# The first mixer's three streams of conditioning weights start behind the input projection's fourth block

## The chip, the core and the metric

One core of a Trainium2 chip runs the whole kernel. The metric is device time of one execution in microseconds (us). The engines are named as in the profile: PE (matmuls), PEld (PE's weight loads), DVE (vector), ACT (scalar activation), POOL (GpSimd) and SP, which issues the DMA loads. Each engine works through its own list of instructions in a fixed order and waits on semaphores for what the others produce.

## What is computed

A decoder trunk of two layers on 256 tokens of width 1024. A layer is a token mixer behind an input projection, then a feed-forward part (dense in the first layer, two of eight experts in the second). Six vectors per layer, made from one conditioning vector, modulate both parts:

```python
cond = silu(c)
for layer in range(2):
    mod = cond @ ada_w[layer] + ada_b[layer]
    shift_mix, scale_mix, gate_mix, shift_ffn, scale_ffn, gate_ffn = split(mod, 6)
    a = rms_norm(h, norm_mix_g[layer]) * (1 + scale_mix) + shift_mix
    z = a @ w_in[layer]        # columns: conv | s5 | stick-breaking | nsa
    h = h + gate_mix * (concat[conv(z), s5(z), stick(z), nsa(z)] @ w_out[layer])
    a = rms_norm(h, norm_ffn_g[layer]) * (1 + scale_ffn) + shift_ffn
    h = h + gate_ffn * (swiglu(a) if layer == 0 else top2of8_swiglu(a))
```

`shift_mix` and `scale_mix` are needed before the input projection. `gate_mix`, `shift_ffn` and `scale_ffn` (the products (0, 2), (0, 3) and (0, 4) below) are needed only behind the first mixer. The s5 part is a linear recurrence: a projection of the state input, two scans over time, an output projection, a gelu and a gate.

## The kernel before

The weight `w_in` is worked through in eleven column blocks of 256. One block is 48 products of 128x128 by 256 (fp32 split into a high and a low part, so three products for each of 16 tiles: lines 291, 292 and 293). Its weights come in one load of 1 MB, of which each half is rounded to the high part on ACT (`wh`) and subtracted on DVE (`wl`, 128x1024); the result stands in a PSUM bank. The pool of PSUM tiles that is called "ps" has two banks, and from the fifth block on every block takes one of them in turn; the pool "acc" has six, for everything else. There are nine buffers for loaded weights (`raw`), four for `wh` and three for `wl`.

Beside the blocks run side streams, Python generators in the list `sides`. `drive(main, sides)` steps each of them once at every `yield` of the main stream, so that they are recorded in small pieces between the products. The main stream of the first mixer writes blocks 0 to 3 (0 is the s5 input), then blocks 6, 7, 4, 5, 8, 9, 10 (`ORDER`), each with four yields. The streams that matter here:

- `s5()`: DVE and ACT copy block 0 into the layout of the recurrence (line 639); 16 small matmuls (line 644) into two banks; on DVE four products, two sums, the scans (lines 656 and 657) and six products and sums that end in the tiles H[0] and H[1]; 24 matmuls into one bank (line 674 on the input, line 676 on H[0] and H[1]); then gelu on ACT, copies on DVE and ACT (line 689), and a gate (line 695 and following).
- `compress()`, `rope()`, `gates()`: other parts of the mixer. `compress()` has its own loads, 32 matmuls (line 732), an activation on ACT and DVE, and two transposes (line 745).
- `extra`: for the first mixer one generator that waits three yields and then makes the three conditioning vectors (0, 2), (0, 3) and (0, 4). Each has four loads of 1 MB (`in_ada_w`), eight fp32 matmuls per load (line 360) and, behind the fourth, an evacuation and a turn into a column (lines 341 to 352, matmuls on line 348). In all 12 loads, 12 MB, and 96 matmuls. For the second mixer `extra` holds the sums for the router (lines 1116 to 1121).

`EV` says which engine empties a block's bank behind it: block 6 ACT, block 7 DVE, block 4 ACT. What is recorded is not yet the order: a scheduler sorts each engine's instructions, and the program is then fixed. Loads are issued by SP in its own order, and one that needs a `raw` buffer still in use holds those behind it.

Of the kernel before, what the change touches and what calls it, by code (L numbers as in the profile page):

```python
# [167 lines left out]
def trunk(ctx: ExitStack, tc: tile.TileContext, I, out):  # L168
# [15 lines left out]
    def s2(shape, dt=F32):  # L184
        return st(shape, "s2", NS2, dt)

    def bank(tag="acc"):
        return ps.tile([128, 512], F32, tag=tag, bufs=NPS[tag], name=nm(tag))
# [13 lines left out]
    def act(o, a, f, **k):  # L202
        S.activation(o, a, f, **k)  # L203
# [27 lines left out]
    def P(l, n, lo=0, hi=None):  # L231
        o, w = SP[n]
        s_, o = (spa[:, l], o) if o < NSA else (sps[l], o - NSA)
        return s_[:, o + lo:o + (w if hi is None else hi)]
# [66 lines left out]
    def run(*gens):  # L301
        for g in gens:
            for _ in g:
                pass

    def drive(main, sides):

        for _ in main:
            for g in list(sides):
                if next(g, 0) == 0:  # L310
                    sides.remove(g)
        while sides:
            for g in list(sides):
                if next(g, 0) == 0:
                    sides.remove(g)
# [254 lines left out]
    def hop(n, l):  # L570
        for _ in range(1 + PAUSE.get((n, l), 0)):
            yield
# [6 lines left out]
    def mixer(l, ah, al, extra=(), second=None, ahead=None):  # L579
# [8 lines left out]
        def prod(c, token, lo=0, hi=KD, tag="ps"):  # L588
            if not lo:
                bk[c] = bank(tag)  # L590
            b = bk[c]
            for j, h, w in stream(I["w_in"][l, c][:, lo:hi]):
                k = lo + j
                for i in range(2):
                    o, c_ = b[:, i * T:(i + 1) * T], slice(i * 128, i * 128 + 128)
                    if token:
                        mm3(o, ah[:, k, c_], al[:, k, c_], h, w, k == 0 and i == 0, k == KD - 1)
                    else:
                        mm3(o, h[:, c_], w[:, c_], ah[:, k], al[:, k], k == 0 and i == 0, k == KD - 1)
                if k % 2:  # L600
                    yield
# [5 lines left out]
        def gates():  # L607
            gwh = s2([128, KD, 12], F32R)
            gwl = s2([128, KD, 12], F32R)
            gw = P(l, "gatew").rearrange("p (k n) -> p k n", k=KD)  # L610
            V.tensor_copy(gwh, gw)
            tt(gwl, gw, gwh.bitcast(F32), OP.subtract)
            pg = bank()
            for k in range(KD):
                mm3(pg[:12, :T], gwh[:, k], gwl[:, k], ah[:, k], al[:, k], k == 0, k == KD - 1)
            gT = st([12, T], "k1", 3)
            act(gT, pg[:12, :T], AF.Tanh, scale=0.5)
            yield from hop("gates0", l)
            pg = bank()
            for t in range(NT):  # L620
                PE.transpose(pg[:, t * 12:t * 12 + 12], gT[:, t * 128:(t + 1) * 128], ident[:12, :12])
            gate = R["gate"] = st([128, NT, 4, 3], "gate")
            V.tensor_copy(gate.rearrange("p t o j -> p (t o j)"), pg[:, :24])
            ts(gate, gate, 0.5, 0.5, OP.mult, OP.add)
            yield
# [148 lines left out]
        def rope_norm(dst, src, tabs, g, tmp):  # L774

            pn, n = src.shape[0], src.shape[1]
            xg, m1, m2 = tmp
            ss = st([128, 8], "ss8", 3)
            act(m1[:pn], src, AF.Square)
            V.tensor_reduce(ss[:pn, :n], m1[:pn], axis=AX.X, op=OP.add)  # L780
            r = rstd(ss[:pn, :n], 8, n, 1.0 / 64)
            tt(xg[:pn], src, g[:pn, None, :].to_broadcast([pn, n, 64]))
            yield from hop("rope_norm0", l)
            m = n // len(tabs)
            for i, (co, si) in enumerate(tabs):
                u = slice(i * m, i * m + m)
                xv, av, bv = (z[:pn, u].rearrange("p n (h d) -> p n h d", h=2) for z in (xg, m1, m2))
                tt(av, xv, co[:pn, None, None, :].to_broadcast([pn, m, 2, 32]))
                tt(bv, xv, si[:pn, None, None, :].to_broadcast([pn, m, 2, 32]))
                tt(xv[:, :, 0], av[:, :, 0], bv[:, :, 1], OP.subtract)  # L790
                tt(xv[:, :, 1], av[:, :, 1], bv[:, :, 0], OP.add)
                yield from hop("rope_norm1", l)
            tt(dst, xg[:pn], r[:pn, :n, None].to_broadcast([pn, n, 64]))


        def rope(c, name, g):
            tmp = [s2([128, 8, 64]) for _ in range(3)]
            qk = s2([128, 8, 64])
            yield from rope_norm(qk, bk[c].rearrange("p (n d) -> p n d", n=8), [(rc[:, t], rs[:, t]) for t in range(NT)],
                                 P(l, g), tmp)  # L800
            p = bank()
            for t in range(NT):
                for b in range(2):
                    PE.transpose(p[:, b * T + t * 128:b * T + t * 128 + 128],
                                 qk[:, t * 4 + 2 * b:t * 4 + 2 * b + 2].rearrange("p a d -> p (a d)"), ident)
            yield from hop("rope0", l)
            R[name] = s2([128, 2, T])
            act(fl(R[name]), p, AF.Copy)
            yield

        def evac(c, name, scale, eng):
            R[name] = s2([128, 2, T])
            if eng == "act":
                act(fl(R[name]), bk[c], AF.Copy, scale=scale)
            else:
                V.tensor_copy(fl(R[name]), bk[c])
            yield
# [52 lines left out]
        def sticks():  # L870
            po = bank()
            for hp in range(2):
                yield from stick(hp, po)
# [105 lines left out]
        def conv_v():  # L979
            R["cv"] = []  # L980
            for c in range(2):
                cv = st([128, T + 2], "cv", 2)
                V.memset(cv[:, 0:2], 0.0)
                tt(cv[:, 2:], bk[9][:, c * T:(c + 1) * T], R["gc"][:, c])
                R["cv"].append(cv)
            yield from hop("conv_v0", l)
            yv = R["yv"] = s2([128, 2, T])
            for c in range(2):
                w = lambda i: P(l, "conv", c * 3 + i, c * 3 + i + 1)
                cv = R["cv"][c]  # L990
                ts(yv[:, c], cv[:, 2:], w(2))
                stt(yv[:, c], cv[:, 1:T + 1], w(1), yv[:, c])
                stt(yv[:, c], cv[:, 0:T], w(0), yv[:, c])
                yield

        def conv_y():
            yv = R["yv"]
            tt(fl(yv), bk[10], fl(yv))
            for c in range(2):
                put_y(c, yv[:, c])  # L1000
            yield

        sides = []

        def main():
            lo = [0] * 4
            if second:
                steps = second()
                for c in range(NB):
                    if c == NA:  # L1010
                        next(steps)
                    run(prod(c, c > 1, 0, 4, "ps" if c < 2 else "acc"))
                    lo[c] = 4
                run(steps)
            yield from prod(0, False, lo[0])
            sides.append(gates())
            sides.append(s5())
            yield from prod(1, False, lo[1])
            sides.append(compress())
            yield from prod(2, True, lo[2])  # L1020
            sides.append(rope(2, "qT", "qg"))
            yield from prod(3, True, lo[3])
            sides.append(rope(3, "kT", "kg"))
            did = set()
            for c in ORDER:
                yield from prod(c, c in (4, 5))
                did.add(c)
                if c in EV:
                    run(evac(c, *EV[c]))
                if c in (4, 6, 7) and did >= {4, 6, 7}:  # L1030
                    sides.append(sticks())
                if c == 5:
                    sides.append(sparse())
                if c in (8, 9) and did >= {8, 9}:
                    sides.append(conv_v())
                if c == 10:
                    sides.append(conv_y())

        EV = {6: ("sq", 0.125, "act"), 7: ("sk", 1.0, "dve"), 4: ("sv", 1.0, "act"), 5: ("nv", 1.0, "act"),
              8: ("gc", 1.0, "act")}  # L1040
        for g in extra:
            sides.append(g)
        drive(main(), sides)

        ahead()
# [529 lines left out]
    def second():  # L1575
        ada_half(0, 1)
        yield
        i = norm(0, "gmix", mod[0, 0], mod[0, 1], old, 4, KD)[3]
        with tc.issue_after(i):
            run(prep)  # L1580
# [57 lines left out]
```

## Time and profile before

| | |
|---|---|
| time before, median of three runs | 1489.4 us (1487.01 to 1490.36) |
| profiled execution, its own time | 1490.53 us |
| its span, first to last instruction | 1488.7 us |
| granted clock of PE, mean over the span | 0.982 |
| busy share of the span: PE, DVE, ACT | 97%, 36%, 24% |
| the input projection of the first mixer and its side streams | about 45 to 195 us of the span |

A granted clock of 1.00 is PE's upper level of 2.4 GHz, 0.50 the lower of 1.2 GHz. Times in a view are in us from the span's first instruction. A view by windows gives, for each stretch of the span, how long each engine was busy; the chain that ended last follows the work back from the end, and shows what released each step; a list of waits gives an engine's idle time by what ended it.

### The profile page before, as it was taken

Reading aid. Unit: us, or ns where it says so; the run is one execution under the profiler, and the core shown is the slowest. Engines: PE = TensorE matmul, PEld = TensorE weight load, DVE = VectorE, ACT = ScalarE, POOL = GpSimd, SP = SyncE. Lnnn points to the kernel's source line nnn. Section 1 sums busy time; section 2 is a strip of 40 time slices with the busy share of each in tenths; the row PEclk is TensorE's granted clock in tenths of the full one; section 3 lists DMA queues with packets and bytes.
Section 4 is the critical chain, followed back from the end, with each engine's and each line's share of the span. In section 5 each row is a group of like instructions: output and inputs, shape, how many; then the busy total and the mean of one; then the engine's idle time right before and its main releaser. Section 6 shows DMA issues by size and latency. Waiting matters only on the chain.

```text
span 1488.7 us, 33596 instructions
## 1 busy us (share of the span) xinstructions
PE 1441.8 (97%) x14802; PEld 899.7 (60%) x14802; DVE 534.5 (36%) x1127; ACT 358.8 (24%) x627; POOL 38.3 (3%) x44
## 2 busy tenths in 40 slices
PE   6999989999999998999999999999999999999996
PEld 4888689999998996734633235545543335445441
DVE  8876568778646865420110010020020020011021
ACT  3436444444444364310100010010010010000010
POOL 1021000000000200000000000000000000000000
PEclk9999999999999998999999999999999999999998
DMA  9985535778755541589899999999999999999996
GB/s 380 382 323 226 207 130 178 266 274 315 284 185 227 226 169 59 208 343 393 337 421 420 421 420 419 419 419 357 406 420 420 420 421 418 420 420 398 420 420 262
DMA packets 69403, 493.30 MB, mean 331 GB/s; under 512 B 8320, under 2 KB 8320, under 8 KB 10240
## 3 DMA queue, kind: packets, MB, share of 16 engines
q1 hardware_dynamic: 69248, 491.06, 82.7%
q8 instruction: 118, 1.93, 0.5%
q14 instruction: 37, 0.30, 0.1%
HBM read 489.98 MB, written 1.05 MB: 330 GB/s over the span
## 4 chain that ended last, share of the span: by engine, by line
PE 85%; DMA 8%; DVE 5%; issue 1%; ACT 1%; POOL 0%; SPq 0%; DVEq 0%; ACTq 0%
PE acc L1276 31%; PE acc L1326 12%; PE ps L291 6%; PE ps L292 6%; PE ps L293 6%; PE acc L291 3%; PE acc L293 3%; PE acc L292 3%; DMA raw<-in_moe_w_down_dram 3%; DMA raw<-in_moe_w_end_dram 3%; PE acc L1319 2%; DMA mix<-in_moe_w_down_dram 1%; DMA yA<-in_moe_w_in_dram 1%; DVE s L197 1%; PE ps L1221 1%; PE ps L1295 1%
## 5 line engine op out<-in xcount | busy, mean ns | idle before, releaser
L1276 PE MATMUL acc<-raw,xt 128*32 128x512 f32 (+1 forms) x3992 | 422.0, 543 | 2.0 <-DMA raw<-in_moe_w_in_dram 1.3
L197 DVE TENSOR_TENSOR s<-acc,s 128x512 f32<-128x512 f32 (+6 forms) x91 | 53.7, 594 | 711.4 <-PE acc L1276 437.7
L1276 PEld LDWEIGHTS acc<-raw,xt 128*32 128x32 f32 x3992 | 138.4, 110 | 207.1 <-issue 168.2
L197 DVE TENSOR_TENSOR wl<-raw,wh 128x1024 fp32r<-128x1024 f32 x144 | 175.9, 1224 | 95.0 <-PE ps L293 58.9
L291 PE MATMUL ps<-ah,wh 128*128 128x256 f32 x672 | 194.0, 290 | 6.1 <-ACT ah L203 5.3
L203 ACT ACTIVATE wh<-raw 128x1024 fp32r<-128x1024 f32 x144 | 152.2, 1061 | 173.1 <-PE ps L292 106.3
L292 PE MATMUL ps<-al,wh 128*128 128x256 f32 x672 | 191.5, 286 | 2.0 <-DVE al L200 2.0
L293 PE MATMUL ps<-ah,wl 128*128 128x256 f32 x672 | 191.4, 285 | 0.0
L1326 PE MATMUL acc<-raw,s 128*32 128x256 f32 x2688 | 174.3, 379 | 0.0
L203 ACT ACTIVATE s<-acc 128x512 f32<-128x512 f32 (+4 forms) x94 | 47.9, 512 | 463.5 <-PE acc L1276 388.1
L1326 PEld LDWEIGHTS acc<-raw,s 128*32 128x32 f32 x2688 | 98.4, 110 | 76.1 <-issue 30.4
L291 PEld LDWEIGHTS ps<-ah,wh 128*128 128x128 f32 x672 | 129.4, 193 | 11.5 <-ACT ah L203 5.7
L292 PEld LDWEIGHTS ps<-al,wh 128*128 128x128 f32 x672 | 129.2, 193 | 3.4 <-DVE al L200 2.5
L293 PEld LDWEIGHTS ps<-ah,wl 128*128 128x128 f32 x672 | 129.2, 192 | 1.6 <-issue 1.6
L203 ACT ACTIVATE s<-ps 128x512 f32<-128x512 f32 (+2 forms) x94 | 42.1, 464 | 253.4 <-PE ps L1295 222.0
L291 PE MATMUL acc<-s,wh 128*128 128x256 f32 x224 | 63.7, 286 | 0.0
L292 PE MATMUL acc<-s,wh 128*128 128x256 f32 x224 | 63.5, 285 | 0.0
L293 PE MATMUL acc<-s,wl 128*128 128x256 f32 x224 | 62.7, 285 | 0.0
L1319 PE MATMUL acc<-raw,s 128*32 128x512 f32 x448 | 57.2, 594 | 1.3 <-DMA raw<-in_moe_w_down_dram 1.3
L203 ACT ACTIVATE s<-s 128x512 fp32r<-128x512 f32 (+6 forms) x50 | 28.3, 569 | 112.8 <-DVE s L197 105.8
L1276 PE MATMUL acc<-yA,xt 128*32 128x512 f32 (+1 forms) x480 | 53.3, 537 | 0.3 <-DMA yA<-in_moe_w_in_dram 0.3
L1276 PE MATMUL acc<-mix,xt 128*32 128x512 f32 (+1 forms) x464 | 51.5, 535 | 0.4 <-DMA mix<-in_moe_w_in_dram 0.4
(368 smaller groups left out, 1664.3 us busy)
## 6 DMA issues: line engine op xcount, KB each, us to landing
raw<-in_moe_w_in_dram SPq DMA_DIRECT2D x145, 1024.0 KB, 15.2
raw<-in_moe_w_down_dram SPq DMA_DIRECT2D x84, 1024.0 KB, 17.4
raw<-in_ada_w_dram SPq DMA_DIRECT2D x48, 1024.0 KB, 7.2
raw<-in_moe_w_end_dram SPq DMA_DIRECT2D x23, 1024.0 KB, 18.3
raw<-in_w_in_dram SPq DMA_DIRECT2D x18, 1024.0 KB, 8.7
yA<-in_moe_w_in_dram SPq DMA_DIRECT2D x17, 1024.0 KB, 14.8
mix<-in_moe_w_in_dram SPq DMA_DIRECT2D x16, 1024.0 KB, 16.5
raw<-in_ffn_w_gate_dram SPq DMA_DIRECT2D x14, 1024.0 KB, 5.0
```

Of the source, the lines that this page charges most:

```text
L197: return V.tensor_tensor(o, a, b, op=op)
L203: S.activation(o, a, f, **k)
L291: PE.matmul(o, lh, rh, start=start, stop=False, skip_group_check=True)
L292: PE.matmul(o, lh, rl, start=False, stop=False, skip_group_check=True)
L293: return PE.matmul(o, ll, rh, start=False, stop=stop, skip_group_check=True)
L1221: PE.matmul(p[:, kk * n:(kk + 1) * n], src[:, t, c], So[:, t, :n], start=(kk == 0 and i == 0 and t == 0), stop=(i == 1 and t == NT - 1), s ...
L1276: PE.matmul(bk[r][32 * j:32 * j + 32, :n], X[:, k, 32 * g:32 * g + 32], v[:, b_], start=(k == 0), stop=(k == KD - 1), skip_group_check=True)
L1295: PE.transpose(p[:, c * 128:(c + 1) * 128], h[0][:, c * 128:(c + 1) * 128], ident)
L1319: PE.matmul(acc[0][32 * j:32 * j + 32], lhs[j % 2], v[:, c % 2, j // 2 * 512:j // 2 * 512 + 512], start=first, stop=last, skip_group_check ...
L1326: PE.matmul(o[32 * j:32 * j + 32], lhs[g], v[:, c % 2, q * 256:q * 256 + 256], start=first and r != 1, stop=last, skip_group_check=True)
```

## The change

The extra streams are no longer put into the list of side streams before the main stream begins. The main stream itself adds them, behind block 3 and before the loop over `ORDER`:

```diff
             yield from prod(3, True, lo[3])
             sides.append(rope(3, "kT", "kg"))
+            sides.extend(extra)
             did = set()
             for c in ORDER:
...
-        for g in extra:
-            sides.append(g)
         drive(main(), sides)
```

The eight yields of blocks 0 to 3 no longer step the extra streams, so every load and matmul of theirs is recorded eight yields later; their number and size stay. On SP the 12 loads move back in the list: in front of the load of block 4's weights stand eleven of them before and four now, and from the load of block 9's weights on the two lists are the same again.

On DVE, between the two scans of the s5 part and the tiles they lead to (lines 656 and 657 are the scans; `s_141` and `s_142` before, `s_134` and `s_135` now, are H[0] and H[1]; `wl_1177` and `wl_1256` are the low parts of block 4's weights). Before:

```order
L656 SCALAR_TENSOR_TENSOR s_123_831<-s_59_329,s_122_830 128x512
L194 TENSOR_SCALAR ms_890<-ss_137_887 128x8
L657 SCALAR_TENSOR_TENSOR s_125_833<-s_59_329,s_124_832 128x512
L197 TENSOR_TENSOR s_122_830<-s_123_831,s_55_316 128x8x63
L197 TENSOR_TENSOR s_133_883<-acc_463,sp_295 128x512
L197 TENSOR_TENSOR s_124_832<-s_125_833,s_56_317 128x8x63
L197 TENSOR_TENSOR s_123_831<-s_123_831,s_56_317 128x8x63
```

Now, from two rows ahead of the first scan:

```order
L197 TENSOR_TENSOR s_120_801<-s_120_801,s_121_802 128x512
L197 TENSOR_TENSOR wl_1177<-raw_1174,wh_1176 128x1024
L656 SCALAR_TENSOR_TENSOR s_119_800<-s_59_329,s_118_799 128x512
L194 TENSOR_SCALAR ms_849<-ss_132_846 128x8
L623 COPY gate_997<-acc_994 128x24
L197 TENSOR_TENSOR s_129_843<-s_128_842,mix_81 128x256 x2
L657 SCALAR_TENSOR_TENSOR s_121_802<-s_59_329,s_120_801 128x512
L197 TENSOR_TENSOR wl_1256<-raw_1174,wh_1255 128x1024
L197 TENSOR_TENSOR s_118_799<-s_119_800,s_55_316 128x8x63
```

Two low parts of weights and the two small steps on `gate` (the second stands a row further down) now stand between the sums and H[1]; before, they stood behind H[1].

On PE, in front of the first matmul on H (line 676). Before (`ps_931` is block 6):

```order
L291 MATMUL ps_931<-ah_113,wh_1046 128x256
L292 MATMUL ps_931<-al_114,wh_1046 128x256
L293 MATMUL ps_931<-ah_113,wl_1047 128x256
L360 MATMUL acc_950<-raw_1116,cond_82 32x256
L676 MATMUL acc_1009<-s_141_912,xt_343 128x64
L360 MATMUL acc_950<-raw_1116,cond_82 32x256 x7
L676 MATMUL acc_1009<-s_142_913,xt_343 128x64
```

Now (`ps_1057` is block 7):

```order
L291 MATMUL ps_1057<-ah_113,wh_1123 128x256
L292 MATMUL ps_1057<-al_114,wh_1123 128x256
L293 MATMUL ps_1057<-ah_113,wl_1124 128x256
L676 MATMUL acc_941<-s_134_865,xt_343 128x64
L676 MATMUL acc_941<-s_135_866,xt_343 128x64
L674 MATMUL acc_941<-s_110_702,mix_81 128x64
```

Between the last matmul on line 644 and the first on line 676 stood 48 products of block 6, half of line 732's matmuls, 25 matmuls on line 360, and a few small ones. Now 22 products of block 6 and all 48 of block 7 stand there with two on line 621, and nothing else.

On PE, behind the last matmul on line 676. Before (`ps_1134` is block 7):

```order
L674 MATMUL acc_1009<-s_110_702,mix_81 128x64
L676 MATMUL acc_1009<-s_141_912,xt_343 128x64
L676 MATMUL acc_1009<-s_142_913,xt_343 128x64
L291 MATMUL ps_1134<-ah_113,wh_1137 128x256
L292 MATMUL ps_1134<-al_114,wh_1137 128x256
L293 MATMUL ps_1134<-ah_113,wl_1138 128x256
```

Now (`ps_1173` is block 4):

```order
L674 MATMUL acc_941<-s_110_702,mix_81 128x64
L676 MATMUL acc_941<-s_134_865,xt_343 128x64
L676 MATMUL acc_941<-s_135_866,xt_343 128x64
L291 MATMUL ps_1173<-wh_1176,ah_113 128x256
L292 MATMUL ps_1173<-wl_1177,ah_113 128x256
L293 MATMUL ps_1173<-wh_1176,al_114 128x256
```

Block 7 stood behind the s5 output; now block 4 stands there, which takes the PSUM bank of block 6. ACT's list around that place has the same rows before and now: the gelu of the s5 output, four copies, the evacuation of `compress()`'s bank, a tanh, and then the evacuation of block 6. In the second mixer the matmuls of the router sums move from the head of the input projection to behind block 3.

## Rows read from the trace of the kernel before

**Rows 1.** The page's part 1: busy time of each engine, share of the span
```profile
PE 1441.8 (97%) x14802; PEld 899.7 (60%) x14802; DVE 534.5 (36%) x1127; ACT 358.8 (24%) x627; POOL 38.3 (3%) x44
```

**Rows 2.** Windows: stretch, its length, each engine's busy us (instructions); clock, DMA share, GB/s
```profile
50.00:75.00 25.00, 25.00 (x240) 19.73 (x239) 19.36 (x47) 11.91 (x27) 0.99 (x2) 0.93 0.93 366
75.00:100.00 25.00, 25.00 (x246) 20.43 (x245) 21.34 (x52) 6.88 (x11) 7.58 (x5) 1.00 0.97 394
100.00:125.00 25.00, 24.61 (x232) 22.80 (x232) 16.03 (x37) 14.67 (x25) 0.54 (x1) 1.00 0.72 285
150.00:175.00 25.00, 23.75 (x181) 14.44 (x181) 15.30 (x54) 12.36 (x39) 0.00 (x0) 1.00 0.64 248
175.00:200.00 25.00, 23.96 (x198) 21.66 (x196) 15.00 (x24) 12.23 (x17) 1.81 (x1) 1.00 0.47 169
```

**Rows 3.** All that PE waited for, 45 to 200 us: total, times, longest
```profile
PE acc L519 <- ACT s L203: 1.0, 1, 1.0
PE ps L292 <- DVE al L200: 1.0, 1, 1.0
PE acc L958 <- DVE s L192: 0.9, 2, 0.7
PE acc L348 <- ACT s L203: 0.4, 1, 0.4
```

**Rows 4.** The chain that ended last, in order of time: start, us, what
```profile
75.60 2.18 PE acc L644 x20
...
89.89 0.55 PE acc L360 x2
90.44 0.36 PE acc L676 x2
...
96.40 0.46 PE acc L676 x4
96.89 0.61 ACT s L203
97.52 0.46 DVE s L689
...
101.17 0.42 DVE s L197
101.62 0.42 ACT s L203
```

**Rows 5.** DVE's instructions by time, 75 to 103 us: start, us, operation, [idle before]
```profile
77.81 1.89 DVE L197 TENSOR_TENSOR s<-acc,s 128x512 f32<-128x512 f32 x3 [0.42 <-PE acc L644]
...
88.71 0.68 DVE L197 TENSOR_TENSOR s<-s,s 128x504 f32<-128x504 f32 x1
...
90.50 0.18 DVE L623 COPY gate<-acc 128x24 f32<-128x24 f32 x1
...
91.39 1.23 DVE L197 TENSOR_TENSOR wl<-raw,wh 128x1024 fp32r<-128x1024 f32 x1
92.52 0.18 DVE L194 TENSOR_SCALAR ms<-ss 128x8 f32<-128x8 f32 x1
```

**Rows 6.** PE's instructions by time, 88 to 108 us, columns as in rows 5
```profile
88.03 0.23 PE L621 MATMUL acc<-cst,k 12*128 12x12 f32 x1
88.19 0.39 PE L291 MATMUL ps<-ah,wh 128*128 128x256 f32 x1
...
96.66 0.37 PE L291 MATMUL ps<-ah,wh 128*128 128x256 f32 x1
96.86 0.28 PE L292 MATMUL ps<-al,wh 128*128 128x256 f32 x1
96.98 0.28 PE L293 MATMUL ps<-ah,wl 128*128 128x256 f32 x1
...
102.32 0.28 PE L293 MATMUL ps<-ah,wl 128*128 128x256 f32 x1
102.99 0.61 PE L348 MATMUL acc<-cst,s 128*128 128x4 f32 x4 [0.39 <-ACT s L203]
```

**Rows 7.** ACT's instructions by time, 70 to 108 us, columns as in rows 5
```profile
102.06 0.60 ACT L203 ACTIVATE s<-ps 128x512 f32<-128x512 f32 x1
```

**Rows 8.** Windows around the clock's falls, columns as in rows 2
```profile
57.20:60.40 3.20, 3.20 (x17) 2.44 (x17) 3.04 (x10) 1.90 (x6) 0.00 (x0) 0.50 0.98 381
196.00:203.80 7.80, 4.09 (x29) 2.21 (x25) 6.22 (x18) 3.88 (x9) 2.46 (x2) 1.00 0.28 116
204.00:210.60 6.60, 5.63 (x26) 5.33 (x26) 4.08 (x10) 2.46 (x7) 0.00 (x0) 0.50 0.01 2
```

**Rows 9.** The page's part 6: loads, KB each, median us from issue to landing
```profile
raw<-in_w_in_dram SPq DMA_DIRECT2D x18, 1024.0 KB, 8.7
```

**Rows 10.** The router's matmuls in the second mixer, 455 to 475 us, by line: busy us, mean ns, idle before
```profile
L1120 PE MATMUL acc<-dg,ones 32*128 32x8 f32 x2 | 0.6, 367 | 0.4 <-DVE dg L192 0.4
```

## The prediction

> **What bounds the kernel now.** I read the busy shares first: PE is busy 97% of the span and no other engine passes 61% [rows 1]. So a change counts only if it moves PE's idle time or its clock, and what a load or a side stream costs elsewhere is free while PE has other work. Then the windows over the first mixer's input projection [rows 2]: PE is busy for 25.00, 25.00 and 24.61 us of three stretches of 25 us, while the loads take 0.93 to 0.97 of the DMA engines until 100 us. A full DMA looks like a second bound; the list of what PE waited for says it is none [rows 3]. From 45 to 200 us there are 3.3 us of waits in these four groups, all on DVE or ACT, none on a load. The order of each engine's instructions is fixed when the program is built, so I followed the one place where the new order differs most from the old: the s5 stream. In the chain that ended last [rows 4] its last projection (line 644) ends at 75.60 + 2.18 = 77.78 us, PE takes up H at 90.44, and the block on H ends at 96.40 + 0.46 = 96.86. The chain runs through PE's own work up to there, then shows gelu, copies and an activation on ACT and DVE, beside which PE was busy with products.
>
> **What the change moves.** Twelve loads, 96 matmuls on line 360 and three turns keep their number and size. PE was full where they stood, so what they took there is given back where they stand now: zero, as long as other work lies over the serial chains of the s5 stream. That is what fails. I count from T, the end of the last matmul on line 644.
>
> *First wait, at line 676.* In the old trace DVE goes from T to H[1] in 88.71 + 0.68 - 77.78 = 11.6 us [rows 5], without a break. The new order puts two low parts of weights into this stretch. One takes 1.23 us, and the next row starts 92.52 - 91.39 = 1.13 us behind it, so 2 x 1.13 = 2.3; the two steps on the gate add about 0.2, and a small sum of 0.07 leaves. H[1] is ready at T + 14.0. Over it lay some 13 us of work on PE (48 products, 16 matmuls on line 732, 25 on line 360 and others: 77.78 to 90.44), and PE took up H without waiting. Now 70 products lie over it, at 0.12 us from start to start (96.86 to 96.98; from 96.86 to 102.32 it is 46 of them) [rows 6], 8.3 us, with two matmuls on line 621 at 0.16 (88.03 to 88.19) and about 0.25 for the changes between kinds: 8.9 us. PE stands at line 676 from T + 8.9 to T + 14.0: **5.1 us**. What could cover it (the rest of line 360, the next block) is queued behind line 676 on PE. Could T move instead? The work ahead of T loses some matmuls of line 360 and gains 16 of line 732 and 20 products; about equal, and a shift of T moves PE's arrival and H alike.
>
> Would a load come late for those two low parts? Block 4's load is the thirteenth that is out of order; its buffer is set free by line 732 about 9 us ahead of T, by the count of PE's rows. With a median of 8.7 us from issue to landing [rows 9] it is there about at T, and DVE comes to it at about T + 4.5. No further wait, with 4 us to spare.
>
> *Second wait, at block 4.* From the end of the block on H at 96.86, ACT and DVE run in sequence gelu, twelve copies, a sum, a tanh (101.62) and then the evacuation of the "ps" bank of block 6, which starts at 102.06 and takes 0.60 [rows 4, 7]: 102.66, or 5.8 us behind line 676. In the old order block 7 covers this: 48 products from 96.66 to 102.44, and only then a wait of 0.39 [rows 6]. In the new order block 7 is used up, and the next block needs the very bank that ACT empties last in its queue. It takes the same 5.8 us with nothing on PE: **5.8 us**, less the **0.4** that was waited there before. The small matmuls of line 745 and the groups of line 360 that would fit in stand behind block 4's first products.
>
> Here a rule of the Trainium skill can be held to the rows. The rows show a block that covers the evacuation of the one before it [rows 6, 7]. The Trainium skill, Perfetto Trace Analysis, section Matmuls, says that independent groups should go round several PSUM banks, so that emptying one lies over the next group's matmuls. The blocks do go round two banks, so by the rule alone this wait would be nothing, the sum 7.1 and the time 1496.5; by the rows it is 5.8, since both banks are full when the block on H begins and ACT's queue empties neither before the tanh.
>
> *Elsewhere.* In the second mixer the router's matmuls leave the head, where the second stage waited 0.4 [rows 10], for a place where products lie beside them: -0.4. Eight of the twelve loads now stand behind block 4's, toward the stretch in which the DMA share is 0.72 instead of 0.97 [rows 2]; no one waited for them at 0.97, so this is worth nothing.
>
> *The clock.* PE's granted clock fell to 0.50 (1.2 GHz, against 2.4 GHz at 1.00) behind stretches in which PE had been idle for much of the time: busy for 4.09 of 7.80 us until 203.8, then at half clock for 6.6 us with 5.63 busy [rows 8]. That fall cost 5.63 / 2 = 2.8 us. The stretch from T + 9 to T + 25 now has 16 us with only the block on H in it (5.2 us), a lower share than that. I take one such fall: **+2.8**. The bounds are 0 (a fall that lies in the waits or none) and 5.6 (two falls, or one that holds both the block on H and the restart). The fall at 57.2 to 60.4 us lies ahead of the change; it cost 1.6 and may go or stay.
>
> The sum: 5.1 + 5.8 - 0.4 - 0.4 + 2.8 = 12.9 us on the profiled execution's 1490.5, so 1503.4. This execution is 1.1 us above the median of the three runs, so the forecast for the median is 1489.4 + 12.9 = **1502 us**.
>
> **The rivals.**
>
> *Both waits, no fall of the clock.* For it: PE has also had gaps without a fall, the 0.39 and the 1.0 us ones of [rows 3]. Against it: these are short. 1489.4 + 10.1 = 1499.5.
>
> *Both waits and more of half clock.* Both the block on H and the restart of block 4 at 1.2 GHz, as in the two ends above: 1489.4 + 10.1 + 5.6 = 1505.
>
> *Only one wait.* The serial chain is shorter than I count (DVE's two low parts fit into breaks, or ACT empties block 6 ahead of the gelu): one of 5.1 and 5.8 goes, and with less idle the clock has less reason to fall: 1489.4 + 5 - 0.4 = 1494, up to 1496. Against it: the order has no breaks on DVE there, and ACT's list has the evacuation behind the tanh.
>
> *Faster: the work moved later fills later gaps.* From 150 to 200 us PE is idle for 1.25 + 1.04, from 196 to 203.8 for 3.7, and the fall of the clock behind it costs 2.8 [rows 2, 8]; with the router's 0.4 that is 9 at most (0.5 is counted twice). If the moved matmuls reached these gaps, and one of the two new waits were not there, the kernel would end at about 1489.4 + 5 - 9 = 1485. It decides at the point where the gaps filled are worth more than the waits. Against it: the last turn of the moved streams is recorded 26 yields into a main stream of 36, ahead of the gaps.
>
> *Faster, by the DMA.* If loads did pace PE while the DMA is at 0.97, taking 12 MB out would help: the waits on DVE and ACT around 45 to 104 us (1.4 us) and the fall at 57 (1.6) would go, 1486 if no new wait came. No row shows PE waiting for a load [rows 3]. The Trainium skill, Perfetto Trace Analysis, section Optimization Strategy, speaks for this case: where the busiest resource changes over time, interleaving the stretches may help. By that rule 1486; the rows leave it little.
>
> *No change.* The new waits lie under something I do not see, or gains and waits cancel: 1489.
>
> **How the numbers follow.** Forecast with one fall (1500.5 to 1504) 0.43; no fall 0.20; more half clock 0.12; one wait alone 0.11; no change 0.07; faster in either way 0.07. The range runs from 1494 (one wait) to 1506 (two falls with 0.5 over), and leaves out the cases of no change and faster and some of the tails. A measurement of this kernel tells apart about 0.2%, 3 us: faster 0.07, same 0.08, slower 0.85.
>
> **What would show it.** In the trace of the changed kernel: PE idle about 5 us in front of the first matmul on line 676, ended by DVE's H; idle about 6 us in front of line 291 on `ps<-wh,ah`, ended by ACT's evacuation of `ps`; the granted clock at 0.5 between these or just behind them; DVE's two rows of `wl` between the scans; the router's wait near 469 gone. If PE waits for a load there instead, my count of buffers is wrong. If the wait at 676 is under 2 us, the cover in front of it was more than 70 products. If both waits are there and the time is still under 1496, the work of line 360 has filled gaps later on.

## The result, and the profile after

The changed kernel takes 1509.9 us (median of 4 runs, 1505.7 to 1510.4) against 1488.4 us before (4 runs, 1487.0 to 1490.4): a ratio of 1.0137, 95% interval 1.0115 to 1.0160. The direction was forecast, the size was not: 1502 was said, with 1506 as the upper end.

Of the changed kernel, the page's part 1, and PE's waits from 40 to 215 us (columns as in [rows 3]):

```profile
PE 1448.6 (96%) x14802; PEld 903.7 (60%) x14802; DVE 533.5 (35%) x1127; ACT 359.1 (24%) x627; POOL 41.3 (3%) x44
```

```profile
PE ps L291 <- ACT s L203: 5.6, 1, 5.6
PE acc L676 <- DVE s L197: 4.6, 2, 3.5
PE acc L958 <- DVE s L192: 1.2, 3, 0.8
```

PE has the same 14802 matmuls and is busy 6.8 us longer in them. Neither of the two waits at the top stands in [rows 3]; they are the two of the prediction. No load is among the waits of this stretch. PE's instructions at the first, from the last matmuls on line 644 on (columns as in [rows 6]):

```profile
75.36 2.34 PE L644 MATMUL acc<-s,xt 128*128 128x64 f32 x20
...
86.15 0.28 PE L293 MATMUL ps<-ah,wl 128*128 128x256 f32 x1
89.88 0.69 PE L676 MATMUL acc<-s,xt 128*128 128x64 f32 x2 [3.46 <-DVE s L197]
91.74 0.69 PE L676 MATMUL acc<-s,xt 128*128 128x64 f32 x2 [1.17 <-DVE s L197]
92.22 0.63 PE L674 MATMUL acc<-s,mix 128*128 128x64 f32 x2
92.65 1.06 PE L676 MATMUL acc<-s,xt 128*128 128x64 f32 x4
...
100.33 1.06 PE L676 MATMUL acc<-s,xt 128*128 128x64 f32 x4
```

DVE's two low parts of weights in the chain ahead of it, and the row that ends in H[1]:

```profile
81.94 1.22 DVE L197 TENSOR_TENSOR wl<-raw,wh 128x1024 fp32r<-128x1024 f32 x1
83.07 1.22 DVE L656 TENSOR_TENSOR_SCAN s<-s,s 128x512 f32<-128x512 f32 x1
...
86.17 1.20 DVE L197 TENSOR_TENSOR wl<-raw,wh 128x1024 fp32r<-128x1024 f32 x1
...
91.01 0.67 DVE L197 TENSOR_TENSOR s<-s,s 128x504 f32<-128x504 f32 x1
```

PE at the second wait, and ACT's emptying of the bank that ends it:

```profile
100.76 0.63 PE L676 MATMUL acc<-s,xt 128*128 128x64 f32 x2
107.02 0.58 PE L291 MATMUL ps<-wh,ah 128*128 128x256 f32 x1 [5.63 <-ACT s L203]
107.40 0.41 PE L292 MATMUL ps<-wl,ah 128*128 128x256 f32 x1
107.61 0.41 PE L293 MATMUL ps<-wh,al 128*128 128x256 f32 x1
107.83 0.41 PE L291 MATMUL ps<-wh,ah 128*128 128x256 f32 x1
```

```profile
106.37 0.60 ACT L203 ACTIVATE s<-ps 128x512 f32<-128x512 f32 x1
```

The block on H runs from 91.74 to 101.39, 9.7 us; four matmuls on line 676 take 1.06 us where [rows 4] show 0.46 of chain for the same group. Products stand 0.21 us apart, not 0.12 as in [rows 6]. That is the lower clock, and the windows show its length (columns as in [rows 2]):

```profile
57.20:60.40 3.20, 3.20 (x31) 2.99 (x31) 3.08 (x5) 1.02 (x4) 0.57 (x2) 1.00 1.04 428
85.00:95.00 10.00, 5.37 (x31) 4.98 (x29) 10.00 (x24) 3.27 (x4) 2.36 (x2) 0.69 0.32 105
95.00:105.00 10.00, 6.39 (x30) 6.20 (x30) 4.85 (x17) 3.28 (x7) 4.79 (x3) 0.50 0.00 0
89.40:113.10 23.70, 16.42 (x83) 14.94 (x83) 12.96 (x38) 7.79 (x13) 5.88 (x3) 0.51 0.09 37
115.00:125.00 10.00, 10.00 (x122) 6.27 (x125) 5.40 (x16) 1.69 (x5) 0.16 (x1) 1.00 0.88 349
```

From 89.4 to 113.1 us the granted clock is 0.51, with 16.42 us of PE work in it. At the upper level that work takes half, so it cost 8.2 us. The early fall of [rows 8] at 57.2 us is not there: -1.6.

The account closes at a fixed point behind the first mixer's projection, the first matmul of line 360 into a "ps" bank. Of before, and of after:

```profile
154.27 0.62 PE L360 MATMUL ps<-raw,cond 128*32 128x256 f32 x2
```

```profile
170.87 1.05 PE L360 MATMUL ps<-raw,cond 128*32 128x256 f32 x10
```

It lies 16.6 us later, with the same 1220 matmuls in front of it. Waits 4.6 + 5.6, less the 0.4 of before, plus 8.2 of half clock, less 1.6 for the early fall: 16.4.

Up to the end 2.8 us more come up (19.4 us between the two spans, 1508.1 and 1488.7). Of these, 1.5 come at one place in the second layer's experts: PE waits 1.8 us for a load there and 0.3 before. The trace of experiment e2, whose first mixer is as before and which runs within 0.1 us of before from 553 to 718 us, has the same row:

```profile
PE acc L1276 <- DMA yA<-in_moe_w_in_dram: 1.7, 1, 1.7
```

So I put that part down to scatter between executions, not to the change. The kernel before itself took 1483.1 to 1493.6 us in its runs beside the experiments, so medians of four carry some 2 us either way; where a trace can be read at the fixed point I use that. Behind that point the traces take from 1329.3 us (e6) to 1339.2 (e4), before 1334.4, the changed kernel 1337.2 and e2 1338.8; so medians and fixed points can differ by some us that these waits don't explain.

### The profile page after: what moved, and what is told of

It is laid out like the page before. It is cut to its first block, busy times and chain, and to the rows that moved or that the text cites. A ratio compares the mean times of both kernels' runs of the same rounds, so it can differ in the third digit from the quotient of the medians.

```text
span 1508.1 us, 33606 instructions
## 1 busy us (share of the span) xinstructions
PE 1448.6 (96%) x14802; PEld 903.7 (60%) x14802; DVE 533.5 (35%) x1127; ACT 359.1 (24%) x627; POOL 41.3 (3%) x44
## 5 line engine op out<-in xcount | busy, mean ns | idle before, releaser
L203 ACT ACTIVATE s<-acc 128x512 f32<-128x512 f32 (+3 forms) x94 | 47.7, 511 | 462.0 <-PE acc L1275 388.4
L203 ACT ACTIVATE s<-s 128x512 fp32r<-128x512 f32 (+6 forms) x50 | 28.1, 568 | 113.0 <-DVE s L197 105.8
## 6 DMA issues: line engine op xcount, KB each, us to landing
raw<-in_moe_w_down_dram SPq DMA_DIRECT2D x84, 1024.0 KB, 17.8
mix<-in_moe_w_in_dram SPq DMA_DIRECT2D x16, 1024.0 KB, 16.4
```

## The experiments

The column "fixed point" is the time of that matmul on line 360, taken from each kernel's trace, against 152.5 us in e2: its first mixer is as before, but without the early fall of the clock. Of the kernels in the table only before has that fall (154.3, so 1.8 in the column). Apart from added ones, the same 1220 matmuls run ahead of the point in each kernel (one more in e4).

| kernel | median us | fixed point, us over e2 | PE waits in front of line 676; behind the block on H |
|---|---|---|---|
| changed | 1509.9 | 18.4 | 4.6; 5.6 |
| e1 first mixer only | 1506.5 | 17.8 | 4.9; 5.6 |
| e3 both filled | 1501.0 | 9.8 | 0.8; 0.9 |
| e4 third bank | 1504.5 | 10.5 | none; 6.7 |
| e5 first filled | 1504.1 | 13.8 | 0.8; 6.5 |
| e6 second filled | 1501.2 | 14.8 | 4.9; 0.7 |
| e7 low parts on POOL | 1507.9 | 19.2 | 5.9; 5.6 |
| e10 behind block 1 | 1495.7 | 10.1 | none; 6.3 |
| e8 behind block 2 | 1492.1 | 6.8 | none; 6.1 |
| e9 behind block 0 | 1491.1 | 4.3 | none; 1.8 |
| e2 second mixer only | 1492.4 | 0 | as before |
| before | 1488.0 to 1490.1 | 1.8 | none; 0.4 |

**Which mixer.** e1 moves the streams in the first mixer alone, e2 in the second alone:

```diff
-            sides.extend(extra)
+            if l == 0: sides.extend(extra)
...
+        if l == 1: sides.extend(extra)
         drive(main(), sides)
```

> The streams move behind block 3 in the first mixer alone; the second mixer keeps its router sums at the head. Theory A (the trace of the changed kernel splits the 19.4 us of span into two waits of 10.2, half clock over the work around them of about 8, less the earlier fall of 1.6, all in the first mixer, and some 2.8 behind it that only follow from where things then fall): about 1507 to 1510, as the changed kernel. Rival B (the 2.8 us behind the first mixer come from moving the router): about 1505 to 1507, and no gain from the router at 465 us.

> The streams move behind block 3 in the second mixer alone (the router sums), the first mixer is as before. Theory A: 1488 to 1489, no change that can be measured, since 0.9 us are saved at the head of the second mixer and about 1.1 come back behind block 3. Rival B: 1490 to 1492.

e1: 1506.5 us, ratio 1.0108 (1.0083 to 1.0134). e2 (with 0 and 1 exchanged): 1492.4, ratio 1.0008 (0.9993 to 1.0023). The loss belongs to the first mixer. The second mixer's move is worth nothing that the medians show: in the changed kernel's trace it saves 0.9 us at its head and loses 1.1 where the router's matmuls now stand; in e2's it saves nothing and loses 1.1. e1's median lies in rival B's range, 0.5 us under theory A's, but its trace rules B out: with the router as before, it too comes up 3.0 us between the fixed point and the end of the span (16.0 and 19.0 us over before; the changed kernel 16.6 and 19.4).

**Is it the idle time that brings the clock down?** e3 gives PE more work in both waits:

```diff
+                if (l, c, k) == (0, 7, KD - 2):
+                    for _ in range(36):
+                        PE.matmul(b[:, :T], al[:, k, :128], w, start=False, stop=False, skip_group_check=True)
...
             pgl = bank()
+            if l == 0:
+                for _ in range(9):
+                    PE.matmul(pgl[:, :256], ident, fl(g4)[:, :256], start=True, stop=True, skip_group_check=True)
```

> The changed kernel with more work on PE: 36 products of low part by low part in block 7 (in front of the first wait, 36 x 0.12 = 4.3 us; they change its sum by less than rounding) and nine matmuls of the identity with the gelu's output into a bank that is overwritten later (in the second wait, 9 x 0.48 = 4.3 us). Theory A (the waits are serial chains of DVE and ACT, and the loss beyond them is PE at half clock because it idles): PE does 8.6 us more work and the kernel is faster than the changed one by some 6 to 9 us, about 1501 to 1504, with a granted clock of 1.0 from 85 to 115 us. Rival C (the half clock has another cause, such as the load of the other engines): as slow as the changed kernel or slower, 1510 to 1518, clock still 0.5 there.

1501.0 us: 8.6 us of work added on the engine that bounds the kernel, and 9 us faster than the changed kernel (5.6 faster than e1 beside it). Windows of e3, where the changed kernel was at 0.51:

```profile
89.40:113.10 23.70, 21.94 (x201) 18.07 (x199) 16.78 (x49) 9.52 (x18) 5.99 (x3) 1.00 0.33 131
```

DVE and ACT do more in this stretch than in the changed kernel, and the clock is 1.00; rival C falls. At the fixed point 9.8 us are left: the added work with the 1.7 us of waits left over is 10.3, less 0.4. Half clock costs nothing any more.

**One wait at a time.** e5 has the first insertion alone, e6 the second alone (it also lets other work in front of block 4).

> The changed kernel with the 36 extra products (low part by low part) in block 7 alone, so that the first wait is filled and the second stays 5.6 us. Theory A: the clock stays at 1.0 until the second wait and falls there; the block on H runs at full clock (5.2 us instead of 9.7) and only the restart of block 4 pays: 1502 to 1505, some 5 us faster than the changed kernel although PE does 4.3 us more. Rival E (the second wait alone decides how long the clock is down): 1506 to 1510.

> The changed kernel with the nine extra matmuls behind the gelu alone (they go to a bank that is overwritten; the order then also puts other work in front of block 4), so that the first wait stays 4.7 us and the second is filled. Theory A: the clock falls at the first wait, about 89 us, the block on H runs at half clock (some 4.5 us lost), and it comes back sooner than at 113 us: 1503 to 1506. If the fall needs both waits: 1499 to 1501, with full clock throughout.

1504.1 and 1501.2 us. Windows of e5, then of e6:

```profile
90.00:95.00 5.00, 4.17 (x38) 4.03 (x37) 5.00 (x17) 3.19 (x3) 1.66 (x1) 1.00 0.18 74
95.00:100.00 5.00, 1.29 (x12) 1.15 (x11) 4.42 (x11) 2.77 (x7) 4.32 (x3) 0.75 0.00 0
100.00:105.00 5.00, 2.21 (x10) 2.21 (x11) 2.29 (x8) 1.01 (x2) 0.00 (x0) 0.50 0.02 5
110.00:115.00 5.00, 5.00 (x75) 3.68 (x73) 0.42 (x1) 0.48 (x3) 0.00 (x0) 1.00 0.76 259
```

```profile
90.00:95.00 5.00, 3.58 (x18) 3.55 (x17) 5.00 (x17) 2.97 (x4) 1.38 (x1) 0.64 0.23 95
95.00:100.00 5.00, 5.00 (x25) 5.00 (x25) 1.75 (x5) 0.48 (x1) 3.25 (x1) 0.50 0.00 0
105.00:110.00 5.00, 5.00 (x34) 3.99 (x36) 1.48 (x5) 1.24 (x3) 0.00 (x0) 1.00 0.00 0
```

Each wait alone comes with a fall, and each time PE's work behind the wait pays. In e5 the fall comes in the second wait, and the block on H runs at 1.00; at the fixed point 13.8 us, of which waits and added work are 0.8 + 4.3 + 6.5 - 0.4 = 11.2, which leaves 2.6 for the clock. In e6 it is 14.8, of which 4.9 + 4.3 + 0.7 - 0.4 = 9.5, which leaves 5.3. Such a remainder holds the order of PE's work too: from 40 us to the fixed point, without added work and with half of the work in the fall taken off, PE is busy for 110.0 us in e6, 111.4 in e2 and 113.0 in e4. The windows of the fall, of e5 and of e6, give the clock without that:

```profile
98.10:108.30 10.20, 5.50 (x34) 4.85 (x37) 4.53 (x13) 2.26 (x6) 1.22 (x2) 0.53 0.01 2
```

```profile
91.80:105.50 13.70, 13.01 (x54) 12.14 (x54) 8.51 (x29) 5.97 (x9) 5.89 (x3) 0.52 0.00 0
```

Half of PE's work in them is 2.8 and 6.5 us. Of e6's, 1.6 are the nine added matmuls (5.75 us there, 4.15 in e3). So the kernel's own work pays 2.8 behind the second wait and some 4.9 behind the first, together about what the changed kernel pays for both (8.2). Rival E and the thought that a fall needs both waits are out. e6's median lies under theory A's range, at the upper edge of the second reading, but its windows show the fall.

**The waits themselves.** e4 takes the first away by giving the blocks a third bank:

```diff
-    NPS = {"ps": 2, "acc": 6}
+    NPS = {"ps": 3, "acc": 5}
```

> The changed kernel with three banks for the blocks and five for the rest. In the order of instructions 48 products of block 4 then stand in front of the first matmul on H, with 70 others; the block behind it still needs the bank that ACT empties last. Theory A: the first wait (4.6 us) is gone, the second (about 5.6) stays, and with it a shorter stretch at half clock: 1497 to 1502. Rival D (each wait alone brings the clock down as far as both): 1503 to 1506. A rule that more banks would take away the second wait: under 1495.

1504.5 us. The first wait is gone, as the 48 products put in front of it say. The second is not: a third bank only lets the order run one block further ahead, and then block 5 needs the bank that ACT empties last. The Trainium skill, Perfetto Trace Analysis, section Matmuls, asks for groups that go round several banks; here that gave no cover by itself, since the emptying stood behind a chain. At the fixed point the waits cost 6.7 - 0.4, and the fall 2.5, half of PE's work in it:

```profile
98.40:108.60 10.20, 4.90 (x25) 4.56 (x29) 4.71 (x14) 2.48 (x7) 2.40 (x3) 0.51 0.28 105
```

The other 1.7 of the 10.5 are PE's longer work at full clock in this order (113.0 us against 111.4). One wait costs less than a third of the clock of both, so rival D is not borne out, though the median lies in its range and 2.5 us above A's: behind the fixed point this trace takes 2.0 us longer than the changed kernel's. Whether that comes from having five banks for everything else isn't shown.

e7 takes the two low parts off DVE:

```diff
-        tt(w, v, h.bitcast(F32), OP.subtract)
+        (eng or V).tensor_tensor(w, v, h.bitcast(F32), op=OP.subtract)
...
-                for j, h, w in stream(I["w_in"][l, c][:, lo:hi]):
+                for j, h, w in stream(I["w_in"][l, c][:, lo:hi], G if (l, c) == (0, 4) else None):
```

> The changed kernel with the two low parts of block 4's weights made by POOL instead of DVE, so that they no longer stand in the chain of DVE to H[1]. Theory A: the first wait shrinks by 2 x 1.13, from 4.6 to 2.3 us, the second stays: 2 to 5 us faster than the changed kernel, 1503 to 1507. If H[1] hangs on anything but DVE's queue: the wait stays 4.6 and the time 1508 to 1510.

1507.9 us, and the wait grew from 4.6 to 5.9. POOL, then DVE in e7, by time:

```profile
80.51 2.39 POOL L277 TENSOR_TENSOR wl<-raw,wh 128x1024 fp32r<-128x1024 f32 x1 [0.87 <-PE ps L293]
86.54 2.78 POOL L277 TENSOR_TENSOR wl<-raw,wh 128x1024 fp32r<-128x1024 f32 x1
```

```profile
81.35 2.10 DVE L197 TENSOR_TENSOR s<-s,s 128x512 f32<-128x512 f32 x1
...
87.05 2.31 DVE L194 TENSOR_SCALAR gate<-gate 128x24 f32<-128x24 f32 x1
```

The same two steps take 0.68 and 0.17 us in the changed kernel. Both end just behind POOL's instruction, at 83.45 and 89.36 against 82.90 and 89.32. So the chain paid for the low parts again, by waiting: 1.4 + 2.1 us, where 2.3 had been saved. This experiment doesn't show what it was made for; that the two low parts cost the chain 2.3 us is shown by DVE's rows alone. The Trainium skill, SBUF — State Buffer, section SBUF: two separate sides, says that DVE and GpSimd share a pair of ports that one holds for a whole instruction, on DVE's side one with two SBUF inputs or in a two-port mode. The 128x512 step, which has two inputs, agrees with that; the 128x24 step has one, and no row shows its mode.

**Where the streams start.** e9, e10 and e8 start them behind block 0, 1 and 2 of the first mixer (one line moved up):

> The streams start behind block 0 in the first mixer, the second as before. In the order 25 matmuls on line 360, 16 on line 732 and 45 products lie over the chain to H, and 24 products of block 7 over the chain to the emptied bank. Theory A: no first wait, a second of about 2 us, too short for the clock to fall by it: 1488 to 1493. Rival F (each later start costs): 1493 to 1500.

> The streams start behind block 1. In the order 84 products, 16 matmuls on line 360 and 12 on line 732 lie over the chain to H (two low parts of weights stand in it on DVE), and behind it comes block 4 with the bank that ACT empties last. Theory A: no first wait, a second of about 6 us, one fall of the clock, as behind block 2: 1490 to 1497. Rival F: between behind block 0 and behind block 2.

> The streams start behind block 2 instead of 3 in the first mixer; the second mixer as before. In the order 60 products, 32 matmuls on line 360 and three on line 732 then lie over the chain to H, and behind it stands block 4, which needs the bank that ACT empties after the tanh and two roundings of weights. Theory A: no first wait, a second of 6 to 8 us, a clock fall shorter than the changed kernel's: 1496 to 1502. Rival F (any start behind the first blocks costs the same, as the loads come late): 1505 to 1510.

1491.1 us (ratio 1.0008, 0.9992 to 1.0023), 1495.7 (1.0039, 1.0025 to 1.0054) and 1492.1 (1.0023, 1.0006 to 1.0040). It is no matter of how late the loads are: later by one block is now dearer, now cheaper. What decides is what the scheduler leaves over the two chains. All three have enough over the first. Over the second e9 has 24 products and six matmuls and waits 1.8 us. e8 and e10 have nothing: e8 waits 6.1 us for a bank (which DVE empties there, not ACT as I expected), e10 6.3 in front of a turn of the moved streams (line 348), behind which block 4 follows:

```profile
PE ps L291 <- DVE s L816: 6.1, 1, 6.1
```

```profile
PE acc L348 <- ACT s L203: 6.3, 1, 6.3
```

Behind e9's 1.8 us too there is a fall (0.50 from 105 to 110 us in its windows), against what I expected. Half of PE's work in the fall is 2.2 us in e8, 3.5 in e10 and 3.4 in e9. That e8 ends 3.6 us ahead of e10 comes up in front of the fixed point (6.8 and 10.1); I can't say why its fall is the shorter one.

These medians lie nearer to before than the fixed points do (2.5, 8.3 and 5.0 us behind before for e9, e10 and e8). All three get 3.3 us back from 254 to 284 us, where before has a fall at 268.8 us and they have none. Windows of before, then of e8:

```profile
245.00:268.60 23.60, 23.60 (x205) 23.60 (x203) 16.70 (x22) 11.35 (x15) 0.00 (x0) 1.00 0.58 211
268.80:275.60 6.80, 6.80 (x34) 6.80 (x34) 4.62 (x9) 3.95 (x11) 0.00 (x0) 0.50 0.53 192
```

```profile
268.80:275.60 6.80, 6.80 (x62) 6.80 (x61) 5.17 (x9) 3.00 (x7) 0.00 (x0) 1.00 0.42 155
```

PE is busy throughout the 23.6 us ahead of that fall, so idle time is not all that a fall can follow.

**Can a filled wait gain on the kernel before?** e11 and e12 are the kernel before with matmuls whose results nobody uses, at the waits in the norms (12 of them), and e12 with eight more in the second mixer's attention:

```diff
         pt = tokens(squares(), "sel8", 1)
         r = rstd(pt[:, :NT], 16, NT, 1.0 / D)
         p = bank()
+        more(3)
         for t in range(NT):
             PE.matmul(p[:, t * 128:(t + 1) * 128], r[:, t:t + 1].to_broadcast([128, 128]), ident, start=True, stop=True)
+        more(3)
```

> The kernel before, with three matmuls on idle columns of a bank on both sides of line 528 in the norm behind the first mixer and in the norm ahead of the second (12 matmuls of 128x256 in all, 0.48 us each; their results are not used), so that PE works through parts of the waits at 200 to 204 and 464 to 468 us. Theory A carried to another place (idling costs the clock, filling it gives that back): the falls at 204 and 467 us go, 2 to 5 us faster than before, 1484 to 1488. If the waits that stay (1.0 us each in front and behind) are enough for the fall: 1488 to 1491.

> The kernel before with the twelve matmuls in the norms as in e11 and eight more of 128x128 (0.22 us each, results not used) in front of line 958 in the second mixer, where PE waits 2.4 us for DVE until 582.8 us. Theory A: the fall at 582.8 us (which costs about 3 us) goes as well, 3 to 6 us faster than before in all, 1484 to 1487. If the fall has its cause in the gap ahead of it at 570 us: as e11, 2 to 3 us faster.

e11: 1487.6 against 1490.1, ratio 0.9985 (0.9969 to 1.0000). Its windows beside [rows 8]:

```profile
196.00:203.80 7.80, 6.43 (x40) 4.09 (x36) 4.92 (x16) 3.02 (x7) 2.25 (x2) 1.00 0.28 118
204.00:210.60 6.60, 4.67 (x24) 4.46 (x25) 5.15 (x12) 3.31 (x8) 0.00 (x0) 0.74 0.01 2
```

The fall behind the first norm is half as long. e12: 1488.8 against 1488.0, ratio 0.9999 (0.9985 to 1.0012), although its profiled run had a mean clock of 0.992 and a span of 1484.7. The mean clock of the runs is higher with the filling (0.985 to 0.992 in e11 and 0.988 to 0.994 in e12, against 0.980 to 0.988 before). Which fall is gone differs between the two, though: e11 keeps part of the one behind the first norm and e12 part of the one behind the second. A gain in time isn't shown.

## Why the prediction was off

- *What bounds the kernel:* right. PE waits for no load where the streams were moved, and the DMA's share there was no bound.
- *First wait, 5.1 us:* 4.6. T is 77.7 (75.36 + 2.34), PE comes to line 676 at 86.4 (T + 8.7; T + 8.9 worked out), H[1] is ready at 91.7 (T + 14.0, as worked out). Of the 5.3 us between, 0.7 are the pair of matmuls on H[0], which runs in the gap.
- *Second wait, 5.8 us:* 5.6.
- *The router, -0.4:* +0.2. It is saved at the head of the mixer (0.9 in the changed kernel) and paid back behind block 3 (1.1).
- *The clock, +2.8 with bounds 0 and 5.6:* 8.2. **This is the step that failed.** I took the length of a fall from one row of before, 6.6 us with 5.63 of work in it, and its double as the upper bound. In that row PE had got back to dense work. Here the fall came in the first wait, the block on H behind it is a run of small matmuls that depend on that wait, and the second wait followed before the clock had come back: it stayed down for 23.7 us. The two ends that I named, the block on H (9.7 us instead of the 5.2 worked out) and the restart of block 4 (half of the 6.1 us from 107.0 to 113.1), are both paid for in full, with the first matmuls on lines 745 and 360 in the restart. Worked out from the work between the waits and behind them, and not from the length of another fall, these two alone come to 7.5.
- *The early fall at 57 us, "may go or stay":* it went, 1.6 us for the change. Against e2, which lacks it too, the cost at the fixed point is 18.4.
- *Behind the fixed point:* 2.8 us came up there, the router's 0.2 among them, where the sum has -0.4: 3.2 too little. On the other side stand the waits, 0.7 shorter than worked out, and the early fall's 1.6. That only 0.9 is left of these is luck; the clock's 5.4 is most of the miss.
- *The rule of the Trainium skill, Perfetto Trace Analysis, section Optimization Strategy, and the rival by the DMA:* no run shows a gain from taking the loads out of the full stretch.

The rival with both waits and more of half clock was the right one; its price was 1505 since it too was capped at two falls of that length. I gave it 0.12.

## What to carry to other kernels

A wait on the engine that bounds the kernel is paid twice here: once as idle time, and again as the work behind it at the lower clock, 2 to 5 us for one wait of 5 to 7 and 8 us for two that stand 10 us apart. When you move work away, look in the order of instructions for what it covered: count the work that is left over each serial chain of the other engines, since the moved work itself costs about the same wherever it stands (PE's 110 to 113 us above). Price the clock by the work that lies between and behind the waits, not by the length of another fall.

## What was not expected

- PE with 8.6 us more work, in the two waits, finished about 9 us sooner (1501.0 against 1509.9). The Trainium skill, TensorE: Matmul & The Clock Gate, section HAM oscillation — how this bites in real kernels, describes work that restarts at the lower clock behind each wait, at a price of half the throttled time. The rows here agree with the restart; the price is half of PE's work in the fall (16.42 us, 8.2 lost), not half of its 23.7 us.
- Which falls a run shows changes between kernels that do the same there: the fall at 57 us is in before, e11 and e12 and in no other trace. It is worth 1.6 us, and the one at 268.8 us 3.3, so a trace should be compared with one that has the same falls. What sets them is open.
- One 128x24 step on DVE, 0.17 us long, took 2.31 us while POOL ran an instruction on 128x1024.
